# Gate and up projections of a feed-forward block as seven block products, with the weight sums made by accumulating DMAs

## The chip, the cores and the metric

The kernel runs on one core of a Trainium2 chip. A core has five engines that run side by side and meet at semaphores: TensorE (PE in the profile, its weight loads PEld), VectorE (DVE), ScalarE (ACT), GpSimd (POOL) and SyncE (SP, which here only issues DMAs). The metric is the device time of one execution in microseconds (us); of the kernel before there are three runs.

## The reference

One step of a two-layer backbone on 640 tokens: 512 of a sample and 128 of a prompt. Each layer is a token mixer (attention of two kinds, pooling, spatial gating), and then the part that matters here, a SwiGLU feed-forward block:

```python
h = rms_norm(x, p["g_pre_ffn"]) * (1.0 + scale2) + shift2
f = (jax.nn.silu(h @ p["w_gate"]) * (h @ p["w_up"])) @ p["w_down"]
x = x + gate2 * rms_norm(f, p["g_post_ffn"])
```

The model width is 1024, the inner width D_FF is 2816, so `w_gate` and `w_up` are 1024 x 2816 each and `w_down` is 2816 x 1024. All is float32.

## The kernel before

**Precision.** A float32 product is made of three products of the tensor engine in its fp32r format (`mm3`, lines 184 to 189): both operands are split into a high part (ACT, line 125) and a low part (DVE or POOL, line 121), and high x high (L187), high x low (L188) and low x high (L189) are added up in PSUM. `hTh` and `hTl` hold the two parts of the transposed, normed and modulated activations: 8 k-tiles of 128 rows, 640 token columns.

**Gate and up.** `ffn` (from line 949) goes through 22 columns blocks f of 128 inner columns. For each it loads two weight chunks of 512 KB (`raw`, 3 buffers, line 172), one of gate and one of up, and splits each in two halves into `wh` and `wl` (8 buffers of 128x512 each). `product` (line 973) then multiplies them with a stretch of token columns, `HALVES`: first 256 columns, then 384. A stretch of one f is 2 weights x 8 k-tiles x 3 = 48 matmuls. The tanh form of silu follows on ACT (L983) and DVE (L984, L985), and the result is split into `ft`, high and low.

**Down.** The f are taken in three groups of 8, 8 and 6. After each group `w_down` of these f is loaded, and 5 token tiles x 2 halves are multiplied (512 columns each) and added into five rows `acc` (L1020 by ACT for the first group, L1022 by DVE for the others).

**Around it.** The last part of the mixer, `tail(t)`, ends the output projection of token tile t (128 tokens; tiles 0 to 4), norms and transposes it (L355 on PE, two halves per tile) and writes its columns of `hTh`/`hTl`. The first products of the feed-forward block stand in PE's queue between these tails. In layer 0, `mods` computes the modulation of layer 1 in the background of `ffn` (L302 on PE, `w_mod` through chunks of 512 KB).

**Order.** The engines take their instructions strictly in the order that the program's scheduler wrote; a DMA is issued by its queue (SP or POOL) in order too, behind the wait for its buffer. The few lines around the products:

```python
order = [(f, hf) for f in fs for hf in range(2)]
if gi == 0:
    order[:4] = [(0, 0), (1, 0), (0, 1), (1, 1)]
...
for j, p in enumerate(banks):
    for k in range(KT):
        wh, wl = w[f][j][k // 4]
        c = slice((k % 4) * 128, (k % 4 + 1) * 128)
        self.mm3(p[:, :nn], (wh[:, c], wl[:, c]), self.hT(k, n0, nn), k == 0, k == KT - 1)
```

Of the kernel before, what the change touches and what calls it, by code (L numbers as in the profile page):

```python
# [16 lines left out]
NT = 5          # token tiles: 4 of the sample, 1 of the prompt  # L17
# [5 lines left out]
HALVES = [(0, 256), (256, 384)]  # L23
GROUPS = [list(range(0, 8)), list(range(8, 16)), list(range(16, 22))]
# [38 lines left out]
class Kernel:  # L63
# [39 lines left out]
    # PSUM: "s2" tiles are two banks, the others one  # L103
# [26 lines left out]
    def rstd(self, out, ss, n, eps=EPS, more=None):  # L130
        """out = (ss + more + n * eps) ** -0.5: the root of n is left to the factor that follows."""
        if more is None:
            self.V.tensor_scalar(out, ss, n * eps, None, op0=ALU.add)  # L133
        else:
            self.V.tensor_scalar(out, ss, more, n * eps, op0=ALU.add, op1=ALU.add)
        self.G.tensor_tensor(out, out, self.mhalf[:, :out.shape[-1]], op=ALU.pow)  # L136

    def rstd2(self, ss):
        """The same of the sum of two halves of a row."""
        r = self.stat(1, "rs")  # L140
        self.rstd(r, ss[:, 0:1], D, more=ss[:, 1:2])
        return r

# [1 line left out]
    def mark(self, engines):  # L145
        """The instructions traced last on the engines."""
# [88 lines left out]
        # the root of D of the norms' factors  # L235
# [46 lines left out]
    def mod(self, l, pair, al, p, bank, part=0, parts=1):  # L282
        """Two vectors, or a part of them: four products at a time, side by side in the columns of the tensor engine."""
# [30 lines left out]
    def ring(self, slots):  # L314
        """Slots in turn; a slot is a tile or a function that allocates one."""
# [20 lines left out]
    def prestat(self, xt, sq, junk):  # L336
        """1 / rms of the rows of xt."""
# [9 lines left out]
    def pre_t(self, xt, r, i, xr, p):  # L347
        """Half i of the columns of xt * r, transposed, in the bank p; xr is work space."""
# [8 lines left out]

    def modulate(self, l, j, t, i, p, ht, eng):
        """Half i of the contraction: scale and shift, then hi and lo, for the columns of token tile t."""
# [8 lines left out]
        sl = slice(t * 128, (t + 1) * 128)  # L368
        self.split(self.hTh[:, 4 * i:4 * i + 4, sl], self.hTl[:, 4 * i:4 * i + 4, sl], ht, eng)
# [22 lines left out]
    def ytile(self, p, nq=0):  # L392
        """The projection in SBUF, its first nq columns (q of B) scaled."""
# [6 lines left out]
    def rope(self, out, src, cos, sin, ns, hd, tmp, e1, e2, e3):  # L400
        """out = src * cos + swap(src) * sin, ns heads of hd; tables [128, hd]."""
# [12 lines left out]
    def k_stack_b(self, k3):  # L414
        """Stack of k of two heads, k3 [128, 4, 32]: slots h, l, h, l of each."""
# [16 lines left out]
    def prep_b(self, l, t, y):  # L432
        """y: [q | k], 4 heads of 2 x 32 each."""
# [39 lines left out]
    def k_stack_a(self, sk, k, eng):  # L473
        """sk [128, 4, 128]: per head hi twice, lo twice; k [128, 128]."""
# [16 lines left out]
    def prep_a(self, l, t, y):  # L491
        """y: [q of 4 heads | k of 2 | v of 2], 64 columns each."""
# [31 lines left out]
    def att1(self, key, t, rv):  # L524
        """Scores and softmax of query tile t; returns the positions that att2 takes."""
# [53 lines left out]
    def att2(self, key, ts, pos, rv):  # L579
        """Products with the values of one or two positions: two token tiles of a head, or two heads of a tile."""  # L580
# [34 lines left out]
    def subln(self, ts):  # L615
        """Norm of each head of B over its 64 columns, for the token tiles ts."""
# [12 lines left out]
    def pool_a(self, t):  # L629
        """Windows' sums minus count * x, transposed, of a token tile."""  # L630
# [39 lines left out]
    def prep_d(self, t, p):  # L670
        """p: PSUM [u | v] before gelu. u and v are kept doubled."""
# [28 lines left out]
    def mix_t(self, parts, ts, k0):  # L700
        """Transposes of 128 columns of the parts (tensor, column) for the token tiles ts into hT from k0 on."""
# [5 lines left out]
        sl = slice(ts[0] * 128, (ts[-1] + 1) * 128)  # L707
# [7 lines left out]
    def mixer_smalls(self, l):  # L715
# [4 lines left out]
        # lambda  # L720
# [12 lines left out]
        # rotary tables times the q / k norm weights  # L733
# [45 lines left out]
    def mixer_e(self, l, first):  # L779
        """Projections of C, the values and q, k of B, and D; pooling and gating."""  # L780
# [85 lines left out]
    def att(self, key=None, ts=None):  # L866
        """An attention step: the softmax runs LAG steps ahead of the products."""
# [10 lines left out]
    def mixer_t(self, l, xsrc, xdst):  # L878
        """Attention of B and the output projection."""
# [5 lines left out]
        def flush(kind, ts):  # L885
            """Attention steps that have to come before a use of their outputs."""
# [16 lines left out]
        def early(n, t):  # L903
            """Half n of the output projection of token tile t but for B."""
# [6 lines left out]
        def tail(t):  # L911
            """The rest of the output projection, and both norms around its end."""
# [8 lines left out]
            self.mix_t([(self.mixB, 0), (self.mixB, 128)], [t], 2)  # L921
            xt = late["x"][t % (1 + TX)]
            self.SY.dma_start(xt, xsrc(t))
            for n in range(2):
                p = self.p("go"[n if t >= TGO else 0])
                self.gemm_tile(p, t, late["w"][n], [8, 9, 2, 3][2 * EARLY[n]:])
                V.tensor_tensor(m[t][n], p, m[t][n], op=ALU.add)
                S.activation(self.ptile()[:, 0:512], m[t][n], AF.Square, accum_out=ss[:, n:n + 1])
            self.postnorm(m[t], ss, late["g"][t // 4], xt, xdst(t), (self.e("pf"), V if t in GV else G))
            self.prenorm(l, 2, t, xt, self.ptile()[:, 0:512], m[t], "pt" if t in PTT else "s2", self.es("pn"))  # L930

        for x in SEQ.split():
# [12 lines left out]
            elif x[0] == "T":  # L945
                for t in x[1:]:
                    tail(int(t))

    def ffn(self, l, xsrc, xdst, last):
        a, T, V, S, G, pa = self.a, self.T, self.V, self.S, self.G, self.pa  # L950
        big = [self.tl(pa, [128, 3, 1024], tag, n) for tag, n in (("kt", 2), ("kt", 2), ("ka", 1))]
        acc = [big[1][:, 0], big[1][:, 1], big[1][:, 2], big[0][:, 0], big[0][:, 1]]
        rows = [big[2][:, 0], big[2][:, 1]]
        xs = [big[0][:, 2], big[2][:, 2]]
        vb = self.tl(pa, [128, 2, 2, 640], "VB", 1, F32R)
        fts = self.ring([lambda: self.tl(pa, [128, 2, 640], "PT", 4, F32R)] * 4 +
                        [lambda: self.tl(pa, [128, 2, 640], "t5", 3, F32R)] * 3 + [vb[:, 0], vb[:, 1]])

        q = self.tl(pa, [128, 2, 1024], "qa", 1)
        if QX[l]:  # L960
            xs += [q[:, i] for i in range(QX[l])]

        def mods():
            if l == 0:
                al = self.mod_alloc(self.ring([q[:, 0], q[:, 1]] + xs[:2] + rows))
                for pair in ((1, 0), (4, 3), (2, 5)):
                    yield from self.mod(1, pair, al, self.pg(), self.pg)
        bg = mods()
        mark = self.mark([V, G, S])
        for gi, fs in enumerate(GROUPS):  # L970
            ft, w = {}, {}

            def product(f, hf, banks):
                n0, nn = HALVES[hf]
                for j, p in enumerate(banks):
                    for k in range(KT):
                        wh, wl = w[f][j][k // 4]
                        c = slice((k % 4) * 128, (k % 4 + 1) * 128)
# [215 lines left out]
```

## Time and profile before

| what | value |
|---|---|
| runs | 1645.87, 1646.59, 1647.8 us; median 1646.59 |
| span of the profiled execution | 1647.5 us |
| PE busy, matmuls | 1588.7 us (96%), 9643 |
| DVE, ACT, POOL busy | 803.2, 662.9, 389.3 us |
| share of PE in the chain that ended last | 83% |
| DMA | 178.50 MB on SP's queue, 32.1% of the 16 engines |

The profiled execution has no time of its own beside its span; the span lies 0.9 us above the median of the runs and inside their range. "Busy" of PE counts overlapping matmuls once, and their ends are modelled, so the pitch (from start to start) is read from the timeline. The feed-forward blocks lie from about 355 to 860 us (layer 0) and from about 1163 us to the end (layer 1).

### The profile page before, as it was taken

To read this page: it belongs to the slowest core of one execution; us is meant where nothing else is said; L and a number is where in the kernel's file an instruction comes from. 1 tells how busy PE (TensorE), PEld (TensorE's weight loads), DVE (VectorE), ACT (ScalarE), POOL (GpSimd) and SP (SyncE) were. 2 spreads that over 40 slices of the span, in tenths; PEclk is the share of its full clock that TensorE was granted. 3 is DMA by queue.
4 is the path that set the end of the run, shared out by engine and by line. 5 is a ranking of instruction groups with operands and counts; after the bars stand their busy time and mean duration, and the time that the engine had idled before them with its cause. 6 is when DMAs were issued, how large, how long until landed. Compare 5 with 4: busy or idle time off the path is not lost.

```text
span 1647.5 us, 24545 instructions
## 1 busy us (share of the span) xinstructions
PE 1588.7 (96%) x9643; PEld 1362.7 (83%) x9643; DVE 803.2 (49%) x1553; ACT 662.9 (40%) x1472; POOL 389.3 (24%) x338
## 2 busy tenths in 40 slices
PE   7999989999999999999999999998899999999998
PEld 5676767678987989889978877776799889988996
DVE  4557777683231223332376687767723222333335
ACT  5343676563222322222254447765523222212222
POOL 3124214552100211021041242254511021101102
PEclk9999999999999999999999999999999999999999
DMA  9854020255453253122242111102422222213212
GB/s 327 307 179 162 29 84 27 78 185 203 165 205 115 90 192 125 56 97 77 71 164 91 55 61 55 39 26 103 167 90 77 71 84 77 68 49 102 77 65 77
DMA packets 62900, 180.08 MB, mean 109 GB/s; under 512 B 9520, under 2 KB 20784, under 8 KB 62784
## 3 DMA queue, kind: packets, MB, share of 16 engines
q1 hardware_dynamic: 62784, 178.50, 32.1%
q8 instruction: 76, 1.25, 0.3%
q14 instruction: 40, 0.33, 0.1%
HBM read 167.17 MB, written 11.30 MB: 108 GB/s over the span
## 4 chain that ended last, share of the span: by engine, by line
PE 83%; DVE 5%; issue 4%; ACT 4%; POOL 3%; DMA 1%; SPq 0%; DVEq 0%; POOLq 0%; ACTq 0%
PE s L187 8%; PE s L188 8%; PE s L189 8%; PE g L187 6%; PE g L189 6%; PE g L188 6%; PE o L187 5%; PE o L188 5%; PE o L189 5%; PE pt L187 5%; PE pt L188 4%; PE pt L189 4%; PE s L302 2%; PE o L602 2%; PE pt L593 2%
## 5 line engine op out<-in xcount | busy, mean ns | idle before, releaser
L121 DVE TENSOR_TENSOR wl<-raw,wh 128x512 fp32r<-128x512 f32 x240 | 189.0, 795 | 351.3 <-ACT wh L125 348.4
L125 ACT ACTIVATE wh<-raw 128x512 fp32r<-128x512 f32 x344 | 212.1, 631 | 342.9 <-PE s L188 153.6
L121 POOL TENSOR_TENSOR wl<-raw,wh 128x512 fp32r<-128x512 f32 x120 | 164.8, 1379 | 719.4 <-ACT wh L125 717.6
L187 PE MATMUL s<-hTh,wh 128*128 128x384 f32 (+1 forms) x928 | 290.0, 313 | 0.0
L188 PE MATMUL s<-hTl,wh 128*128 128x384 f32 (+1 forms) x928 | 289.0, 311 | 0.0
L189 PE MATMUL s<-hTh,wl 128*128 128x384 f32 (+1 forms) x928 | 288.3, 311 | 0.0
L187 PEld LDWEIGHTS s<-hTh,wh 128*128 128x128 f32 x928 | 174.4, 188 | 6.1 <-ACT P L983 4.2
L189 PEld LDWEIGHTS s<-hTh,wl 128*128 128x128 f32 x928 | 174.6, 188 | 0.0
L188 PEld LDWEIGHTS s<-hTl,wh 128*128 128x128 f32 x928 | 174.2, 188 | 0.2
L187 PE MATMUL pt<-hTh,wh 128*128 128x384 f32 (+1 forms) x448 | 140.1, 313 | 4.0 <-ACT hTh L125 3.9
L188 PE MATMUL pt<-hTl,wh 128*128 128x384 f32 (+1 forms) x448 | 139.6, 312 | 0.0
L189 PE MATMUL pt<-hTh,wl 128*128 128x384 f32 (+1 forms) x448 | 138.8, 310 | 0.0
L187 PE MATMUL g<-wh,hTh 128*128 128x512 f32 x256 | 106.5, 416 | 0.6 <-ACT hTh L125 0.5
L188 PE MATMUL g<-wl,hTh 128*128 128x512 f32 x256 | 103.8, 405 | 0.0
L189 PE MATMUL g<-wh,hTl 128*128 128x512 f32 x256 | 103.3, 404 | 0.4 <-DVE hTl L121 0.4
L136 POOL TENSOR_TENSOR rs<-rs,mhalf 128x1 f32<-128x1 f32 (+3 forms) x66 | 58.2, 885 | 176.8 <-DVE rs L133 126.9
L187 PEld LDWEIGHTS pt<-hTh,wh 128*128 128x128 f32 x448 | 84.5, 189 | 7.7 <-ACT hTh L125 5.1
L547 DVE TENSOR_REDUCE nm<-s 128x1 f32<-128x640 f32 x96 | 77.5, 820 | 27.0 <-PE s L546 13.9
L548 ACT ACTIVATE P<-s,nm 128x640 f32<-128x640 f32 x96 | 76.3, 797 | 28.8 <-DVE nm L547 27.4
L189 PEld LDWEIGHTS pt<-hTh,wl 128*128 128x128 f32 x448 | 84.8, 189 | 0.0
L188 PEld LDWEIGHTS pt<-hTl,wh 128*128 128x128 f32 x448 | 84.4, 188 | 0.3 <-DVE hTl L121 0.3
L984 DVE SCALAR_TENSOR_TENSOR P<-P,s 128x384 f32<-128x384 f32 (+1 forms) x58 | 28.2, 486 | 101.2 <-ACT P L983 101.2
(370 smaller groups left out, 3177.9 us busy)
## 6 DMA issues: line engine op xcount, KB each, us to landing
raw<-in_w_gate SPq DMA_DIRECT2D x44, 512.0 KB
raw<-in_w_up SPq DMA_DIRECT2D x44, 512.0 KB
raw<-in_w_down SPq DMA_DIRECT2D x44, 512.0 KB
kt<-in_w_mod SPq DMA_DIRECT2D x40, 512.0 KB
raw<-in_w_in SPq DMA_DIRECT2D x32, 512.0 KB
ka<-in_w_mod SPq DMA_DIRECT2D x24, 512.0 KB
raw<-in_w_out SPq DMA_DIRECT2D x16, 512.0 KB
qa<-in_w_mod SPq DMA_DIRECT2D x16, 512.0 KB
```

The lines of the kernel that those rows point to most:

```text
L121: eng.tensor_tensor(lo, src, hi.bitcast(F32), op=ALU.subtract)
L125: self.S.activation(hi, src, AF.Copy)
L136: self.G.tensor_tensor(out, out, self.mhalf[:, :out.shape[-1]], op=ALU.pow)
L187: self.T.matmul(out, ah, bh, start=first, stop=False)
L188: self.T.matmul(out, ah, bl, start=False, stop=False)
L189: self.T.matmul(out, al, bh, start=False, stop=last)
L302: self.T.matmul(p[32 * j:32 * j + 32, 0:w], self.c2[:, c:c + 32], raw[k][j // 2][:, j % 2 * w:(j % 2 + 1) * w], start=c == 0, stop=c == 2 ...
L547: V.tensor_reduce(nm[:, s:s + 1], sc[:, :, :320], axis=AX.XY, op=ALU.max, negate=True)
L548: S.activation(P[s].rearrange("p (a b) -> p a b", a=2), sc[:, :, :320], AF.Exp, bias=nm[:, s:s + 1], accum_out=sm[:, s:s + 1])
L593: T.transpose(p[:, j - j0, i * 128:(i + 1) * 128], P[:, j * 128:(j + 1) * 128], self.ident)
L602: T.matmul(o[64 * i:64 * i + 64, 0:128], vt[:, j if nkt == 5 else 5], PT[:, j, i * 128:(i + 1) * 128], start=j == 0, stop=j == nkt - 1)
L984: V.scalar_tensor_tensor(ta, ta, 1.0, gp, op0=ALU.add, op1=ALU.mult)
```

## The change

The 22 blocks f become 11 pairs. Pair 0 is multiplied as before, but with two equal token halves of 320 columns (`HT`). For each of the other ten pairs the product of activations and weights is seen as blocks: the activations A in 2 x 2 (token halves x halves of the 1024 rows), the weights in four blocks b0 to b3 (halves of the rows x the two f of the pair; each block holds gate and up side by side, 128x1024). Instead of eight block products there are seven, numbered 1 to 7, each of 2 banks x 4 k-tiles x 3 matmuls of 320 columns (`product`, new). Their operands are A11 with b0 (product 1), A22-A21 with b0+b1 (5), A12 with b2 (2), a signed sum of A blocks with b0+b1+b3 (6), another with b3 (3), A11-A21 with b1+b3 (7) and A22 with b0+b1+b2+b3 (4); they stand in the order 1, 5, 2, 6, 3, 7, 4, and the 4 of a pair stands behind the 1 of the next.

What this needs beside the products:

- `combine`: the sums of activations, made once per layer on DVE and split by ACT and DVE, for three stretches of columns. For that the token tiles get other columns (`cols`): the first 320 columns hold tiles 0, 1 and the first half of tile 2.
- `blocks`: the sums of weights. `raw` u is loaded with b0 and split; then an accumulating DMA issued by POOL adds b1 to it in place, the sum is split again, b3 is added, split, b2 is added, split. A second `raw` v does b3, then b3+b1. b2 alone comes through two `s` tiles. So a pair has 3 plain loads, 4 accumulating DMAs (512 KB each) and 7 splits of 128x1024, where two f before had 4 loads and 8 splits of 128x512. An accumulating DMA waits for the split ahead of it, and the split behind it waits for the DMA.
- Splits of these weights go to ACT and DVE alone (before, every second low part went to POOL). `wh` and `wl` are 4 buffers of 128x1024 instead of 8 of 128x512.
- In `middle` and `end`: five additions of 128x640 on DVE per pair, PSUM to SBUF (L1138, L1163), between the products and the silu (`swiglu`, L1063 to L1066).
- Four groups for the down projection (2, 3, 3, 3 pairs) instead of three; `w_down` and, in layer 0, `w_mod` come through the eight `s` tiles of 128x512 (before: 512 KB chunks), the latter spread over groups 1 to 3, three steps per pair (`mod_s`).

```diff
-HALVES = [(0, 256), (256, 384)]
-GROUPS = [list(range(0, 8)), list(range(8, 16)), list(range(16, 22))]
+HT = TOK // 2
+GROUPS = [[0, 1], [2, 3, 4], [5, 6, 7], [8, 9, 10]]
...
+    def piece(self, src):
+
+        h, l = self.wtile()
+        for x in src:
+            c, y = x
+            self.split(h[:, c], l[:, c], y, self.V)
+        return h, l
+
+    def blocks(self, l, pair):
+
+
+        SY, G = self.SY, self.G
+        blk = [self.a["w_gu"][l, pair, q] for q in range(4)]
+        full = slice(0, 1024)
+        wraw = lambda: self.tl(self.wp, [128, 1024], "raw", 3)
+        add = lambda o, q: G.dma_start(o, blk[q], accum_op=ALU.add)
+        u = wraw()
+        SY.dma_start(u, blk[0])
+        yield self.piece([(full, u)])
+        add(u, 1)
+        yield self.piece([(full, u)])
+        z = [self.s() for _ in range(2)]
+        for i in range(2):
+            SY.dma_start(z[i], blk[2][:, i * 512:(i + 1) * 512])
+        add(u, 3)
+        yield self.piece([(slice(i * 512, (i + 1) * 512), z[i]) for i in range(2)])
+        yield self.piece([(full, u)])
+        add(u, 2)
+        v = wraw()
+        SY.dma_start(v, blk[3])
+        yield self.piece([(full, v)])
+        add(v, 1)
+        yield self.piece([(full, v)])
+        yield self.piece([(full, u)])
...
+            V.tensor_tensor(a22, a22, a21, op=ALU.subtract)
+            self.split(*out(5), a22, V)
+            V.tensor_tensor(a21, a11, a21, op=ALU.subtract)
+            V.scalar_tensor_tensor(a11, a22, -1.0, a11, op0=ALU.mult, op1=ALU.subtract)
+            self.split(*out(6), a11, V)
+            self.split(*out(7), a21, V)
+            V.scalar_tensor_tensor(a12, a12, -1.0, a11, op0=ALU.mult, op1=ALU.subtract)
+            late.append((out(3), a12))
...
+    def product(self, n, w, banks, first=True, last=True):
+
+        ah, al = self.ops[n]
+        wh, wl = w
+        for j, p in enumerate(banks):
+            o = p[:, 0:HT]
+            for k in range(4):
+                c = slice(j * 512 + k * 128, j * 512 + (k + 1) * 128)
+                a, b = (wh[:, c], wl[:, c]), (ah[:, k, :], al[:, k, :])
+                self.T.matmul(o, a[0], b[0], start=first and k == 0, stop=False, skip_group_check=True)
+                self.T.matmul(o, a[0], b[1], start=False, stop=False, skip_group_check=True)
+                self.T.matmul(o, a[1], b[0], start=False, stop=last and k == 3, skip_group_check=True)
...
+            self.product(5, next(w), [b[:, 0], b[:, 1]], last=False)
+            add(wt, b, x)
+            self.product(2, next(w), aa, first=False)
+            self.swiglu(t1[:, n1], aa[0][:, n1], aa[1][:, n1], 1, 0)
+            next(bg, None)
+            self.product(6, next(w), [c[:, 0], c[:, 1]], last=False)
+            add(yt, c, x)
+            next(bg, None)
+            self.product(3, next(w), [b[:, 0], b[:, 1]], first=False)
+            add(yt, b, yt)
+            self.swiglu(t2[:, n1], yt[:, n1], yt[:, n2], -1, 0)
+            next(bg, None)
+            self.product(7, next(w), [c[:, 0], c[:, 1]], first=False, last=False)
+            add(wt, c, wt)
+            self.swiglu(t2[:, n2], wt[:, n1], wt[:, n2], -1, 1)
...
+            for pair in ps:
+                if pair == 0:
+                    continue
+                nst = begin(pair)
+                if st:
+                    end(st)
+                st = nst
+                middle(st, bg)
```

Two places show how instructions move. The first is PE at the start of the feed-forward block of layer 0: `s_762`/`s_810` are the transposes of token tile 2, `pt_37..` those of tile 3, `o_37..` the end of tile 4's and 3's output projection, and `s_799`/`s_851` the first gate product. Before:

```order
L355 MATMUL s_810_3679<-identr_77,s_2500 128x128 x4
L189 MATMUL o_3803<-wh_3431,hTl_89 128x512
L187 MATMUL s_851_3884<-hTh_88,wh_3865 128x256
L188 MATMUL s_851_3884<-hTl_89,wh_3865 128x256
L189 MATMUL s_851_3884<-hTh_88,wl_3866 128x256
...
L355 MATMUL pt_3756<-identr_77,s_2502 128x128 x4
L355 MATMUL pt_3757<-identr_77,s_2503 128x128 x3
L355 MATMUL s_810_3679<-identr_77,s_2501 128x128 x4
L355 MATMUL pt_3757<-identr_77,s_2503 128x128
L189 MATMUL s_851_3884<-hTh_88,wl_3880 128x256
```

and now:

```order
L371 MATMUL s_762_3631<-identr_77,s_2468 128x128 x4
L192 MATMUL o_3755<-wh_3381,hTl_89 128x512
L371 MATMUL pt_3708<-identr_77,s_2470 128x128 x4
L371 MATMUL pt_3709<-identr_77,s_2471 128x128 x4
L371 MATMUL s_762_3631<-identr_77,s_2469 128x128 x4
L190 MATMUL s_799_3834<-hTh_88,wh_3813 128x320
L190 MATMUL g_3890<-hTh_88,wh_3824 128x320
L190 MATMUL o_3891<-hTh_88,wh_3824 128x320
L191 MATMUL s_799_3834<-hTl_89,wh_3813 128x320
```

Before, 41 products of 256 columns stood ahead of the transposes of tile 3; now all transposes of tiles 2 and 3 stand ahead of the first product, which reads columns of tile 2.

The second place is DVE in the middle of a group, layer 0. Before, a pair of low parts of weights (`wl`) stands between the silu of one stretch and the next, each waiting for a chunk that depends on nothing else:

```order
L121 TENSOR_TENSOR wl_4595<-raw_4588,wh_4594 128x512
L121 TENSOR_TENSOR wl_4605<-raw_4598,wh_4604 128x512
L984 SCALAR_TENSOR_TENSOR P_4421<-P_4421,s_902_4372 128x384
L985 SCALAR_TENSOR_TENSOR P_4421<-P_4421,s_902_4372 128x384
L121 TENSOR_TENSOR PT_4315<-P_4421,PT_4315 128x384
L984 SCALAR_TENSOR_TENSOR P_4509<-P_4509,s_915_4460 128x256
```

Now, with `raw_4787` the u of one pair and `raw_5073` that of the next (L1138 adds a product from PSUM):

```order
L121 TENSOR_TENSOR wl_5031<-raw_4983,wh_5030 128x1024
L121 TENSOR_TENSOR wl_5076<-raw_5073,wh_5075 128x1024
L1138 TENSOR_TENSOR P_4858<-s_926_4856,P_4786 128x640
L121 TENSOR_TENSOR wl_5106<-raw_4787,wh_5105 128x1024
L1138 TENSOR_TENSOR P_4858<-s_925_4855,P_4858 128x640
L121 TENSOR_TENSOR wl_5149<-raw_5073,wh_5148 128x1024
L1064 SCALAR_TENSOR_TENSOR P_4860<-P_4860,P_4858 128x320
L1066 SCALAR_TENSOR_TENSOR P_4860<-P_4860,P_4858 128x320
L1138 TENSOR_TENSOR P_4857<-s_926_4856,P_4857 128x640
```

`wl_5076` is the split for product 1 of the next pair; the accumulating DMA of b1 goes out behind it, and `wl_5149`, which waits for that DMA, stands three rows on, ahead of the addition that frees the bank of product 7 (`s_926`) for product 4. On POOL nothing but these DMAs is left inside the feed-forward block, in order (x3: three on the same u):

```order
L996 DMA raw_4787<-in_w_gu 128x1024 x3
L996 DMA raw_4983<-in_w_gu 128x1024
L996 DMA raw_5073<-in_w_gu 128x1024 x3
L996 DMA raw_5269<-in_w_gu 128x1024
L996 DMA raw_5652<-in_w_gu 128x1024 x3
```

Before, POOL made half of the low parts of weights there.

## Rows read from the trace of the kernel before

**Rows 1.** The page: busy time by engine; the last chain by engine.

```profile
PE 1588.7 (96%) x9643; PEld 1362.7 (83%) x9643; DVE 803.2 (49%) x1553; ACT 662.9 (40%) x1472; POOL 389.3 (24%) x338
...
PE 83%; DVE 5%; issue 4%; ACT 4%; POOL 3%; DMA 1%; SPq 0%; DVEq 0%; POOLq 0%; ACTq 0%
```

**Rows 2.** Stretches: length, PE, PEld, DVE, ACT, POOL busy, clock, DMA share, GB/s.

```profile
0.00:60.00 60.00, 49.54 (x423) 34.54 (x424) 28.16 (x75) 27.84 (x62) 19.30 (x25) 1.00 0.97 321
...
360.00:840.00 480.00, 478.49 (x2899) 428.82 (x2898) 152.39 (x271) 138.83 (x265) 70.00 (x54) 1.00 0.38 131
```

**Rows 3.** PE's groups by line and shape: count, busy us, mean ns.

```profile
L187 PE MATMUL s<-hTh,wh 128*128 128x384 f32 x480 | 162.7, 339 | 0.0
...
L187 PE MATMUL s<-hTh,wh 128*128 128x256 f32 x448 | 127.4, 284 | 0.0
```

**Rows 4.** PE's timeline, layer 0: start, us, line, operands, shape.

```profile
525.33 0.40 PE L189 MATMUL o<-wh,PT 128*128 128x512 f32 x1
...
546.33 0.40 PE L187 MATMUL g<-wh,VB 128*128 128x512 f32 x1
...
548.16 0.28 PE L187 MATMUL s<-hTh,wh 128*128 128x256 f32 x1
...
553.20 0.28 PE L187 MATMUL s<-hTh,wh 128*128 128x256 f32 x1
...
553.73 0.34 PE L187 MATMUL s<-hTh,wh 128*128 128x384 f32 x1
...
558.50 0.34 PE L187 MATMUL s<-hTh,wh 128*128 128x384 f32 x1
```

**Rows 5.** Timelines of PE, ACT and DVE at the start of layer 0's block.

```profile
355.20 0.28 PE L187 MATMUL s<-hTh,wh 128*128 128x256 f32 x1
...
361.36 0.98 PE L355 MATMUL pt<-identr,s 128*128 128x128 f32 x7 [1.08 <-DVE s L352]
...
364.11 0.69 DVE L121 TENSOR_TENSOR hTl<-s,hTh 128x512 fp32r<-128x512 f32 x1
...
370.33 1.15 ACT L125 ACTIVATE hTh<-s 128x512 fp32r<-128x512 f32 x2
...
371.04 2.71 POOL L121 TENSOR_TENSOR hTl<-s,hTh 128x512 fp32r<-128x512 f32 x2 [3.19 <-ACT hTh L125]
...
371.98 1.46 PE L302 MATMUL g<-ka,c 128*32 128x512 f32 x10
```

**Rows 6.** The same place in layer 1: timelines, PE's longest wait, one stretch.

```profile
1162.93 0.36 PE L187 MATMUL s<-hTh,wh 128*128 128x256 f32 x1
...
1173.15 0.62 ACT L125 ACTIVATE hTh<-s 128x512 fp32r<-128x512 f32 x1
...
1180.16 0.63 ACT L125 ACTIVATE hTh<-s 128x512 fp32r<-128x512 f32 x1
...
PE pt L187 <- ACT hTh L125: 3.9, 1, 3.9
...
1180.00:1185.00 5.00, 1.94 (x6) 1.94 (x7) 3.16 (x8) 3.49 (x9) 3.62 (x3) 0.75 0.15 57
```

**Rows 7.** Instructions on `raw` (ns min/median/max), DVE groups (count, busy us, mean ns).

```profile
L121 DVE TENSOR_TENSOR wl<-raw,wh x240: 676/693/1798, 20.0 to 1619.7; 128x512 fp32r<-128x512 f32 x120
...
L573 DVE SCALAR_TENSOR_TENSOR P<-P,rb,P 128x640 f32<-128x640 f32 x24 | 23.6, 984 | 1.0
...
L984 DVE SCALAR_TENSOR_TENSOR P<-P,s 128x384 f32<-128x384 f32 x30 | 16.4, 548 | 0.0
...
L984 DVE SCALAR_TENSOR_TENSOR P<-P,s 128x256 f32<-128x256 f32 x28 | 11.8, 421 | 101.2 <-ACT P L983 101.2
```

**Rows 8.** Two 512 KB loads: issue on SP, and the ACT split that waited.

```profile
1482.21 0.33 SPq L172 DMA_DIRECT2D raw<-in_w_down  x1
...
1485.87 1.16 ACT L125 ACTIVATE wh<-raw 128x512 fp32r<-128x512 f32 x2 [1.62 <-DMA raw<-in_w_down]
...
23.19 0.34 SPq L172 DMA_DIRECT2D raw<-in_w_in  x1
...
30.90 1.15 ACT L125 ACTIVATE wh<-raw 128x512 fp32r<-128x512 f32 x2 [1.36 <-DMA raw<-in_w_in]
```

**Rows 9.** The page: the only DMA queue of loads: packets, MB, share.

```profile
q1 hardware_dynamic: 62784, 178.50, 32.1%
```

More of the change, by code (lines that the diff above doesn't have):

```diff
@@ L329, in mod_alloc, with mod_s @@
         return al
+    def mod_s(self, l, pair, p, bank):
+        src = self.a["w_mod"][l].rearrange("(k p) (i n) -> p k i n", p=128, n=D)
+        for k in range(KT):
+            for j in range(4):
+                raw = self.s()
+                self.SY.dma_start(raw, src[:, k, pair[j // 2], j % 2 * 512:(j % 2 + 1) * 512])
+                self.T.matmul(p[32 * j:32 * j + 32], self.c2[:, 2 * k:2 * k + 32], raw, start=k == 0, stop=k == KT - 1)
+            yield
+        self.mod_finish(l, pair, 512, 0, p, lambda what: self.s(), bank)
+        yield
     def row(self, l, i, c, tile_):
@@ L947, in mixer_t @@
                     tail(int(t))
-    def ffn(self, l, xsrc, xdst, last):
-        a, T, V, S, G, pa = self.a, self.T, self.V, self.S, self.G, self.pa
[L951 to L978, printed above, removed]
-                        self.mm3(p[:, :nn], (wh[:, c], wl[:, c]), self.hT(k, n0, nn), k == 0, k == KT - 1)
-                gp, up = (p[:, :nn] for p in banks)
-                ta = self.ptile()[:, :nn]
-                sl = slice(n0, n0 + nn)
-                S.activation(ta, gp, AF.Tanh, scale=0.5)
-                V.scalar_tensor_tensor(ta, ta, 1.0, gp, op0=ALU.add, op1=ALU.mult)
-                V.scalar_tensor_tensor(ta, ta, 0.5, up, op0=ALU.mult, op1=ALU.mult)
-                self.split(ft[f][:, 0, sl], ft[f][:, 1, sl], ta)
-            order = [(f, hf) for f in fs for hf in range(2)]
-            if gi == 0:
-                order[:4] = [(0, 0), (1, 0), (0, 1), (1, 1)]
-                first = list(FIRST)
-                self.n3 = 2
-            for f, hf in order:
-                if hf == 0:
-                    w[f] = [self.chunk(a[nme][l, f], self.es("wg")) for nme in ("w_gate", "w_up")]
-                    ft[f] = next(fts)
-                product(f, hf, self.pair(first.pop(0) if first else ("s2", "s2", "pt")[self.n3 % 3]))
-                self.n3 += 1
-                if hf:
-                    self.step(bg, PACE, mark)
-            lastg = gi == len(GROUPS) - 1
-            if lastg:
-                self.step(bg, 99, mark)
-                rows = [self.row(l, 5, c, rows[c]) for c in range(2)]
@@ new lines, in combine, with rest @@
+    def combine(self, m):
+        V = self.V
+        kt = [self.tl(self.pa, [128, 2, 4, HT], "kt", 2, F32R) for _ in range(2)]
+        s3 = [self.tl(self.pa, [128, 4, HT], "PT", 4, F32R) for _ in range(2)]
+        h, lo = self.hTh, self.hTl
+        self.ops = {1: (h[:, 0:4, 0:HT], lo[:, 0:4, 0:HT]), 2: (h[:, 4:8, 0:HT], lo[:, 4:8, 0:HT]),
+                    3: (h[:, 0:4, HT:TOK], lo[:, 0:4, HT:TOK]), 4: (h[:, 4:8, HT:TOK], lo[:, 4:8, HT:TOK]),
+                    5: (kt[0][:, 0], kt[0][:, 1]), 6: (kt[1][:, 0], kt[1][:, 1]), 7: s3}
+        late = []
+        for c, t1, t2 in ((256, 2, 2), (0, 0, 3), (128, 1, 4)):
+            n = 64 if t1 == 2 else 128
+            q = lambda t, i, o: m[t][i].rearrange("p (k n) -> p k n", n=128)[:, :, o:o + n]
+            o2 = 64 if t1 == 2 else 0
+            a11, a12, a21, a22 = q(t1, 0, 0), q(t1, 1, 0), q(t2, 0, o2), q(t2, 1, o2)
+            out = lambda k: [x[:, :, c:c + n] for x in self.ops[k]]
+            V.tensor_tensor(a22, a22, a21, op=ALU.subtract)
[6 more added lines that the diff above has]
+            late.append((out(3), a12))
+        def rest():
+            for o, x in late:
+                self.split(*o, x, V)
+        return rest
@@ L1005, in ffn @@
                 ss = [self.stat(2, "ss2") for _ in range(NT)]
             for n in range(2):
[L1007 removed]
+                w = []
+                for pair in ps:
+                    h, lo = self.wtile()
+                    for i in range(2):
+                        c = slice(i * 512, (i + 1) * 512)
+                        x = self.s()
+                        self.SY.dma_start(x, a["w_down"][l, n, pair][:, c])
+                        self.split(h[:, c], lo[:, c], x, V)
+                        w.append((h[:, c], lo[:, c]))
```

151 lines of the change are left out of this document (128 added, 23 removed).

## Prediction

> **What bounds the kernel now.** The busy times and the last chain came first [rows 1]: PE is busy 96% of the span and is 83% of the chain that ended last, and no other engine passes 49%. So time follows from the columns that PE works through, as long as nothing makes it wait. The stretches come second [rows 2]: in the feed-forward block of layer 0 PE works 478.49 of 480 us, at a full granted clock, with the DMA engines at 0.38. The groups by shape [rows 3] tell how much of that is gate and up: 448 to 480 matmuls a line in these two groups alone; with the other PSUM tags there are 704 of each shape in each of the three lines (11 pairs, 2 layers, 2 f, 2 weights, 8 k), so 2112 of 256 columns and 2112 of 384. The means there (284 and 339 ns) count the drain of a pipelined matmul, so the pitch must come from the timeline [rows 4]: (553.20−548.16)/42 = 0.120 us for 256 columns, (558.50−553.73)/27 = 0.177 for 384, (546.33−525.33)/90 = 0.233 for 512. The pitch is proportional to the columns within 3%.
>
> **What is removed and added on PE.** 320 columns do not occur among these rows; I take the mean of 256 and 384, 0.148 us. (From below 0.146, 512's rate; from above 0.150, 256's; over the 3744 matmuls counted next that is ±8 us.) Before: 2112 × (0.120+0.177) = 626 us. After: pair 0 has 2 halves × 2 f × 2 weights × 24 = 192 matmuls a layer, 28.4 us, 57 us for both. A product has 24 matmuls, 3.56 us, and a pair seven, 24.9 us; 20 pairs are 497 us. Together 554: **72 us less**, 3.6 for each of the 20 pairs. Columns for the down projection and the modulation stay.
>
> **The engines behind it.** DVE per pair: 7 low parts of 128x1024, 14 × 0.693 = 9.7 us; five additions of 640 columns at about 0.85 (below the 0.984 of a three-operand one) 4.3; silu, eight instructions of 320 columns at about 0.485, 3.9; low parts of the result 1.8 [rows 7]. That is 19.7 of 24.9 us, high but no bound. ACT: 7 × 1.16 = 8.1 for the high parts [rows 8] and about 4 for the rest. POOL loses its splits. What gets thin is the lead: the split weights hold four products, 14.2 us, where eight chunks held 28.5.
>
> **The accumulating DMAs.** No such DMA is in the trace: SP's queue is the only one with loads [rows 9]. The question is A, from the end of a split to the landing of the sum. From below it is a plain 512 KB load at a quiet place, 1485.87−1482.21 = 3.66 us; among many loads 30.90−23.19 = 7.7 [rows 8]. From above, twice that, 15.4. A second read of 512 KB takes 1.5 us at the engines' rate: 131/0.38 = 345 GB/s, and 321/0.97 = 331 [rows 2], over the whole run 178.5 MB/(0.321 × 1647.5 us) = 337 [rows 9]. I take 3.7+1.5 and some 0.8 for issue by POOL: A = 6 quiet, 8.5 beside `w_mod`.
>
> The Trainium skill gives a price for the plain transfer: "DMA: Bandwidth & Descriptors", section "Anatomy of one DMA — SWDGE (gpsimd) path", 2.0 us and bytes/436 GB/s, so 3.2 us for 512 KB as an estimate, 0.5 under the quiet row here. "Collectives: The Full Stack", under "Why ReduceScatter is half of AllGather", says that an add is held to half rate because it reads two sources on one ring; that would make 4.4 us of it, with which no pair would stall and the sum below would be 1598. No row here shows either.
>
> How much A can hide: the split for the next pair's product 1 finds its buffer free when product 2 has ended. Product 4 follows four products later (6, 3, 7 and the next 1), 14.2 us. Between lie that split (1.16 on ACT, 1.39 on DVE), A, the split of the sum (2.55), two steps of silu (1.0) and the addition that frees product 7's bank for product 4 (1.0), since DVE works strictly in order. 14.2−7.1 leaves **A up to 7.1 us hidden**; each us more costs one per pair. At 3.6 us gain per pair, an A of about 10.7 takes all of it.
>
> So layer 1 hides the adds (6 against 7.1). In the nine pairs of layer 0 with `w_mod`, a pair moves 7 × 0.524 MB of weights, 12 × 0.262 of `w_mod`, and 4 × 0.524 read back for the sums: 8.9 MB in 24.9 + 12 × 0.146 [rows 5] = 26.6 us, 335 GB/s, the capacity above. Hence 8.5 there: 1.4 over, 9 pairs, **13 us lost**.
>
> **The start of the block.** Before, PE had 96 products of 256 columns, 11.5 us, that need tiles 0 and 1 alone; it ran them from 355.20 while tiles 2 to 4 were normed [rows 5]. Now the first product reads half of tile 2. That tile's first half is split low by 364.80; the second, by the high part at 370.33 and the low part behind it, is ready near 372. With the first half 48 matmuls can run, 7.1 us, so 4.4 of the 11.5 are bared; the place also holds 2.8 us of modulation (ten take 1.46) and late low parts such as POOL's, 3.19 late. I take 8 us. In layer 1 products began at 1162.93, the halves are split near 1173.8 and 1181, and before PE waited 3.9 us there too, after which the clock was granted at 0.75 [rows 6]; 11.5−7.1 = 4.4, I take 5. **13 us lost**, from 6 (all but the bared part hidden) to 20 (no product before the second half, 11.5 in each, less 3).
>
> **First pairs and groups.** In each layer the first of the seven-product pairs finds its buffers still held by pair 0, and its chain of split, A, split runs bare in part: 3 us each, **6 us** (0 to 2 × 8.5). A fourth group adds a round of waits and ten additions of 512 columns on DVE, up to 7 us; in the third group's stretch down matmuls stood in step [rows 4], so it can be 0; **4 us**.
>
> **Sum.** −72+13+13+6+4 = −36. Against the profiled 1647.5 that is 1611.5; this execution lies 0.9 us above the median of the runs, which gives **1611**.
>
> **Rivals.**
> *The adds cost nothing.* If A stays under 7.1 also beside `w_mod` and the first pairs are covered: −72+13+4 = −55, 1592. For it: the engines have 0.38 share now, and the quiet load is 3.66. Against: 335 GB/s in those pairs.
> *The engines saturate in layer 0.* If a sum takes their time three times (source, old value, write), a pair needs 11.0 MB, at 345 GB/s 31.9 us, 5.3 more than PE: 48 us instead of 13, about 1646, no change. For it: in the first 60 us the share was 0.97 and PE was idle for 10 of them [rows 2]. Against: the 0.38 was counted with each byte once, so reads and writes seem to overlap.
> *Slow adds, the other side.* If issue on POOL and the sum make A 12 us everywhere, then 5 us of stall in 18 pairs, 90 instead of 13 and 6: about 1682, slower. It decides from A = 10.5. For it: 7.7 for a plain load under load, and each pair chains three sums on one buffer. Against: POOL has nothing else to do there. The skill bears on this rival with "DMA: Bandwidth & Descriptors", section "SWDGE vs HWDGE vs iDMA": descriptors from GpSimd are written by it into SBUF, where VectorE in its two-port mode can lock it out. No row here shows it.
> *The pitch of 320 is no mean.* Weight loads average 1362.7/9643 = 0.141 us [rows 1], hardly under 0.148; if they showed, all 3744 matmuls would be dearer. But 256 columns go at 0.120 with the same loads [rows 4], so it is worth at most the 8 us above.
>
> **Chances.** The sum as worked out 0.45, free adds 0.2, saturation 0.15, slow adds 0.18; 0.02 for the rest. The first case has 1590 to 1630 of its own (start 6 to 20, pitch ±8, taken together). The range must also hold the first two rivals: 1586 to 1655; slow adds are left out. A measurement of this kernel tells 0.2% (3.3 us) from no change. Faster: 0.45+0.2 and a third of saturation and a little, 0.71; same 0.07; slower 0.22.
>
> **What would show it.** Right: gate and up matmuls at a pitch near 0.148 and products of 3.56 us back to back in layer 1; a PE wait of some us ahead of the first product in each layer, ended by ACT or DVE on tile 2; short waits before product 4 in layer 0's pairs with `w_mod`, ended by the chain from a POOL DMA; A of 6 and 8.5. Wrong: PE waits of over 3.6 us in every pair, in layer 1 too (A over 10.5); a DMA share near 1 through layer 0's block (saturation); DVE above 90% there, with additions, not splits, ending PE's waits.

## The result: slower, with the adds as cheap as forecast

The changed kernel takes 1714.19 us (median of 4 runs, 1710.76 to 1715.36), the kernel before 1646.23 beside it: ratio 1.0397, interval 1.0378 to 1.0417. The forecast was 1611, with 1586 to 1655 as the range and a chance of 0.22 for slower. The slow-adds rival (1682) has the right sign, but not the right reason, as the rows show.

From the page of the changed kernel: busy times, the queue of POOL's DMAs, and the DMA issues with their median from issue to landing.

```profile
PE 1565.2 (91%) x9163; PEld 1314.6 (77%) x9163; DVE 1002.8 (59%) x1825; ACT 721.7 (42%) x1508; POOL 347.5 (20%) x330
...
q0 software_dynamic: 11520, 41.95, 13.8%
...
raw<-in_w_gu POOLq DMA_DIRECT2D x80, 512.0 KB, 6.0
raw<-in_w_gu SPq DMA_DIRECT2D x48, 512.0 KB, 3.7
```

Beside [rows 1], PE is busy 23.5 us less, where 72 were forecast, and idle 147.8 us of 1713.0 instead of 58.8 of 1647.5. The accumulating DMA, POOL's row, takes 6.0 us in the median, just what was taken for the quiet case.

Where did PE wait? Three rows of PE's waits, over the whole span: who ended them, total us, times, longest.

```profile
PE s L1056 <- ACT wh L125: 25.6, 14, 5.0
PE s L1056 <- DVE P L1138: 18.9, 12, 2.4
...
PE pt L1056 <- ACT wh L125: 8.7, 4, 4.4
```

L1056 is the first matmul of each three of a product. The waits end with the high part of a weight sum (ACT) or with an addition (DVE) that stands behind a split in DVE's queue. What those wait for shows in one pair of layer 1, where no `w_mod` is loaded. ACT's splits of `raw` and POOL's DMAs, from one split of product 7 to the next (start, us, xcount, idle time before and its releaser), then the stretch as in [rows 2]:

```profile
1346.00 2.96 ACT L125 ACTIVATE wh<-raw 128x1024 fp32r<-128x1024 f32 x3 [4.37 <-DMA raw<-in_w_gu]
1356.01 1.06 ACT L125 ACTIVATE wh<-raw 128x1024 fp32r<-128x1024 f32 x1 [7.05 <-DMA raw<-in_w_gu]
1364.42 1.06 ACT L125 ACTIVATE wh<-raw 128x1024 fp32r<-128x1024 f32 x1 [3.60 <-DMA raw<-in_w_gu]
1366.69 1.05 ACT L125 ACTIVATE wh<-raw 128x1024 fp32r<-128x1024 f32 x1
1376.11 1.06 ACT L125 ACTIVATE wh<-raw 128x1024 fp32r<-128x1024 f32 x1 [4.54 <-DMA raw<-in_w_gu]
...
1349.86 0.90 POOL L996 DMA_DIRECT2D raw<-in_w_gu  x1 [8.78 <-DVE wl L121]
1358.73 0.89 POOL L996 DMA_DIRECT2D raw<-in_w_gu  x1 [7.97 <-DVE P L1064]
1367.14 0.88 POOL L996 DMA_DIRECT2D raw<-in_w_gu  x1 [7.53 <-DVE wl L121]
1370.15 0.88 POOL L996 DMA_DIRECT2D raw<-in_w_gu  x1 [2.13 <-DVE P L1064]
...
1346.00:1376.10 30.10, 26.13 (x172) 24.96 (x171) 17.18 (x26) 10.80 (x17) 3.53 (x4) 1.00 0.54 122
```

Read it as a chain. At 1346.00 ACT splits, one behind the other, the weights of products 7, next 1 and 4. The split of next 1 lets b1 go out at 1349.86; its sum is split for product 5 at 1356.01 (6.15 us). That lets b3 go out at 1358.73, split for 6 at 1364.42 (5.69). Behind it, ACT splits v for product 3 at 1366.69; that lets b1 go out into v at 1370.15, split for 7 at 1376.11 (5.96), and only behind that, in the order of ACT, stands the split for the next product 1. So a turn is **three accumulating DMAs in a row**, 17.8 us, and 12.3 us of splits and order between them: 30.11 us, where PE has work for 24.7 (shown below, in the kernel without a chain). PE is busy 26.13 of these 30.10 us, at a granted clock of 1.00. The fourth DMA, of 1367.14, lies beside the third.

In layer 0 the DMAs take longer beside `w_mod` (8.2 and 9.1 us, from issue to split, around the waits below). There, a wait can cost twice (PE's timeline around product 5 of one pair and product 4 of the pair before, then the stretch, and layer 0 as in [rows 2]):

```profile
655.71 0.31 PE L1058 MATMUL pt<-hTh,wl 128*128 128x320 f32 x1
...
657.03 0.31 PE L1058 MATMUL pt<-hTh,wl 128*128 128x320 f32 x1
659.77 0.64 PE L1056 MATMUL s<-kt,wh 128*128 128x320 f32 x1 [2.43 <-ACT wh L125]
...
662.69 0.63 PE L1056 MATMUL s<-hTh,wh 128*128 128x320 f32 x1 [2.02 <-DVE P L1138]
663.12 0.47 PE L1057 MATMUL s<-hTl,wh 128*128 128x320 f32 x1
663.39 0.47 PE L1058 MATMUL s<-hTh,wl 128*128 128x320 f32 x1
...
659.00:666.00 7.00, 4.21 (x14) 3.81 (x15) 5.38 (x10) 3.97 (x8) 0.86 (x1) 0.53 0.69 175
...
360.00:840.00 480.00, 441.18 (x2572) 384.35 (x2572) 239.20 (x381) 157.35 (x259) 43.83 (x46) 0.96 0.58 157
```

After the waits of 2.43 and 2.02 us the pitch is 663.39−663.12 = 0.27 us instead of (657.03−655.71)/9 = 0.147: the granted clock of that stretch is 0.53, so close to its lower level of 1.2 GHz. Over the same 480 us as in [rows 2], PE is busy 441.18 us instead of 478.49 and the mean clock 0.96 instead of 1.00.

### The profile page after: what moved, and what is told of

Its sections match the earlier page's. It is cut to its first block, busy times and chain, and to the rows that moved or that the text cites. A ratio compares the mean times of both kernels' runs of the same rounds, so it can differ in the third digit from the quotient of the medians.

```text
span 1713.0 us, 24194 instructions
## 1 busy us (share of the span) xinstructions
PE 1565.2 (91%) x9163; PEld 1314.6 (77%) x9163; DVE 1002.8 (59%) x1825; ACT 721.7 (42%) x1508; POOL 347.5 (20%) x330
## 3 DMA queue, kind: packets, MB, share of 16 engines
q1 hardware_dynamic: 76608, 168.02, 28.5%
q0 software_dynamic: 11520, 41.95, 13.8%
## 5 line engine op out<-in xcount | busy, mean ns | idle before, releaser
L121 DVE TENSOR_TENSOR wl<-raw,wh 128x1024 fp32r<-128x1024 f32 (+1 forms) x192 | 208.3, 1102 | 297.6 <-ACT wh L125 297.3
L125 ACT ACTIVATE wh<-raw 128x1024 fp32r<-128x1024 f32 (+1 forms) x208 | 177.5, 889 | 380.1 <-DMA raw<-in_w_gu 265.1
L1056 PE MATMUL s<-kt,wh 128*128 128x320 f32 x320 | 101.9, 318 | 19.0 <-ACT wh L125 18.9
L1056 PE MATMUL s<-hTh,wh 128*128 128x320 f32 x320 | 104.6, 327 | 12.2 <-DVE P L1138 11.1
L1056 PE MATMUL pt<-hTh,wh 128*128 128x320 f32 x320 | 101.4, 317 | 8.8 <-ACT wh L125 8.7
L1058 PE MATMUL s<-kt,wl 128*128 128x320 f32 x320 | 99.8, 312 | 4.4 <-DVE wl L121 4.4
L1058 PE MATMUL s<-hTh,wl 128*128 128x320 f32 x320 | 102.4, 320 | 0.8 <-DVE wl L121 0.7
L1057 PE MATMUL s<-hTl,wh 128*128 128x320 f32 x320 | 102.2, 319 | 0.0
L1057 PE MATMUL pt<-hTl,wh 128*128 128x320 f32 x320 | 100.6, 315 | 0.0
L1057 PE MATMUL s<-kt,wh 128*128 128x320 f32 x320 | 99.5, 311 | 0.0
L1056 PEld LDWEIGHTS s<-kt,wh 128*128 128x128 f32 x320 | 60.4, 189 | 29.6 <-ACT wh L125 21.8
L1056 PEld LDWEIGHTS s<-hTh,wh 128*128 128x128 f32 x320 | 63.6, 199 | 23.1 <-DVE P L1138 12.9
```

What stands on the lines that cost most here:

```text
L121: eng.tensor_tensor(lo, src, hi.bitcast(F32), op=ALU.subtract)
L125: self.S.activation(hi, src, AF.Copy)
L1056: self.T.matmul(o, a[0], b[0], start=first and k == 0, stop=False, skip_group_check=True)
L1057: self.T.matmul(o, a[0], b[1], start=False, stop=False, skip_group_check=True)
L1058: self.T.matmul(o, a[1], b[0], start=False, stop=last and k == 3, skip_group_check=True)
```

## The experiments

**Theories.** The chain: a pair can't be shorter than three accumulating DMAs in a row and the splits between them. VectorE: it has 59% of the span instead of 49%, works in order, and ends a third of the waits above; its amount of work is what costs. Traffic: the second read of the sums fills the DMA engines in layer 0. And the prediction's own reading: only the DMA between next product 1 and next product 5 counts, and 7 us of it are hidden.

**No add, same places** (the sums are left out):

```diff
-        add = lambda o, q: G.dma_start(o, blk[q], accum_op=ALU.add)
+        add = lambda o, q: G.dma_start(o, blk[q])
```

> The four DMAs that POOL issues per pair load their block without adding it, into the same buffers and behind the same splits; the sums of weights are left out. Chain theory: a pair's period is three of these DMAs in a row plus about 12.3 us of splits between them (29.7 us in layer 1 now, with 5.6 to 6.2 us each from issue to split). If a plain one takes 4.5 us, the period is 25.8 in layer 1, just above the 24.9 of PE, and the time falls from 1714 to about 1640 to 1655. VectorE theory (PE waits because VectorE takes its splits and additions in one order and has too many of them): that work is unchanged, so the time stays at 1705 to 1715. Traffic theory (the second read of the sums fills the DMA engines in layer 0): layer 0 alone gains, some 45 us, layer 1 keeps its 29.7 us periods: about 1670.

Measured: 1618.9 us (1618.67 to 1625.75), ratio 0.9833 [0.9806, 0.9859]. From its page:

```profile
q0 software_dynamic: 11520, 41.95, 7.7%
...
raw<-in_w_gu POOLq DMA_DIRECT2D x80, 512.0 KB, 4.1
```

And the first matmul of the first and of the last product 7 in layer 1:

```profile
1218.19 0.31 PE L1056 MATMUL s<-PT,wh 128*128 128x320 f32 x1
...
1562.14 0.31 PE L1056 MATMUL s<-PT,wh 128*128 128x320 f32 x1
```

The DMA from POOL takes 4.1 us instead of 6.0, and 95 us go; the order on PE, VectorE, ScalarE and GpSimd is that of the changed kernel. More than expected, since 4.1 is under the 4.5 that was assumed. VectorE's theory fails, as its work is unchanged (1004.7 us). The traffic theory fails too: between these two products 7 of layer 1 lie 344.0 us, where the changed kernel has 389.2 (its lines stand under "Why the prediction was wrong"), while in layer 0 this distance falls by 34.7.

**No chain** (the sums are left out; every split has a buffer that SP loads plain):

```diff
-        u = wraw()
-        SY.dma_start(u, blk[0])
-        yield self.piece([(full, u)])
-        add(u, 1)
-        yield self.piece([(full, u)])
+        def one(q):
+            u = wraw()
+            SY.dma_start(u, blk[q])
+            return self.piece([(full, u)])
+        yield one(0)
+        yield one(1)
...
```

> Every one of the seven splits reads a block that SyncE loaded plain into a buffer of its own turn; no DMA waits for the split before it, and the sums of weights are left out. All matmuls, splits and additions on VectorE stay. Chain theory: PE sets the pairs again, 24.9 us in layer 1 and about 28.5 with its modulation in layer 0; the 90 us or so of waits and slow clock inside the groups go: 1610 to 1630. VectorE theory: 1700 to 1715. Traffic theory: layer 0 gains up to 45 us, layer 1 nothing: about 1670.

Measured: 1597.37 us (1596.36 to 1598.97), ratio 0.9689 [0.9675, 0.9704]; below what any theory gave, nearest to the chain. Its busy times, a stretch of layer 1, and the first matmul of product 7 in two pairs of it:

```profile
PE 1523.0 (95%) x9163; PEld 1289.1 (81%) x9163; DVE 1007.8 (63%) x1825; ACT 725.8 (45%) x1508; POOL 276.1 (17%) x250
...
1258.00:1310.00 52.00, 52.00 (x355) 51.90 (x354) 38.46 (x60) 24.56 (x40) 0.00 (x0) 1.00 0.44 151
...
1258.24 0.31 PE L1051 MATMUL s<-PT,wh 128*128 128x320 f32 x1
1282.89 0.30 PE L1051 MATMUL s<-PT,wh 128*128 128x320 f32 x1
```

A pair takes 24.65 us here, PE doesn't stop in this stretch, and VectorE has the same work as in the changed kernel (1007.8 against 1002.8), 74% of the stretch. This kernel also tells what the adds and the waits for them cost in all: 1713.0−1595.7 = 117.3 us, of which 147.8−72.7 = 75.1 are idle time of PE and 1565.2−1523.0 = 42.2 are busy time of PE for the same 9163 matmuls. The lower clock is a part of these 42.2: the mean granted clock is 0.963 in the changed kernel and 0.982 here, which is at most 0.037 × 1713.0 − 0.018 × 1595.7 = 34.7 us. The rest was not taken apart.

**Another order** (nothing left out): the next pair's product 1, with its split and DMA, stands ahead of product 7. For that, the sums of b1 into u and into v are also issued ahead of products 1 and 3 instead of behind them.

```diff
-        yield self.piece([(full, u)])
+        w = self.piece([(full, u)])
         add(u, 1)
+        yield w
...
             next(bg, None)
+            nst = begin(nxt) if nxt else None
             self.product(7, next(w), [c[:, 0], c[:, 1]], first=False, last=False)
...
```

> Product 1 of the next pair, and with it its split and accumulating DMA, stands ahead of product 7 of this pair in the program (order 1, 5, 2, 6, 3, next 1, 7, 4); nothing is added or left out. Chain theory: the DMA for product 7 and that for the next product 5 then run side by side, and the period is two DMAs and about 9 us: 21 us in layer 1, 25 in layer 0, under PE's 24.9 and 28.5. The time falls to 1620 to 1645. VectorE theory: same work, other order: within 10 us of 1714. If each DMA could hide 7 us as the prediction had it, the order would also not matter: 1714.

Measured: 1642.83 us (1640.1 to 1644.82), ratio 0.9963 [0.995, 0.9976]; inside what the chain theory gave, near its upper end, 71 us under the changed kernel. ACT and POOL in layer 1:

```profile
1308.32 1.06 ACT L125 ACTIVATE wh<-raw 128x1024 fp32r<-128x1024 f32 x1 [1.52 <-PE s L1059]
1313.60 1.06 ACT L125 ACTIVATE wh<-raw 128x1024 fp32r<-128x1024 f32 x1 [3.23 <-DMA raw<-in_w_gu]
1318.63 1.06 ACT L125 ACTIVATE wh<-raw 128x1024 fp32r<-128x1024 f32 x1 [2.46 <-PE s L1059]
...
1307.28 0.88 POOL L996 DMA_DIRECT2D raw<-in_w_gu  x1 [1.34 <-DVE wl L121]
1311.56 0.90 POOL L996 DMA_DIRECT2D raw<-in_w_gu  x1 [3.40 <-DVE P L1066]
```

The split for next 1 (1308.32) no longer waits for the sum for 7 (issued 1307.28, split 1313.60), and it and the one for next 5 (1318.63) wait for a buffer that PE frees, no more for a DMA. The two sums run side by side.

**GpSimd adds** (nothing left out): the blocks come into spare `s` tiles by SP, and GpSimd adds them.

```diff
-        add = lambda o, q: G.dma_start(o, blk[q], accum_op=ALU.add)
+        def add(o, q):
+            for i in range(2):
+                c, y = slice(i * 512, (i + 1) * 512), self.s()
+                SY.dma_start(y, blk[q][:, c])
+                G.tensor_tensor(o[:, c], o[:, c], y, op=ALU.add)
```

> The blocks to be added are loaded by SyncE into spare 128x512 tiles ahead of time, and GpSimd adds them, two additions of 128x512 per sum, in the place of the accumulating DMA; order as in the change. GpSimd's subtractions of that shape took 1.38 us before, so a sum takes about 2.9 us. Chain theory: period 3 x 2.9 + 12.3 = 21 us, under PE's: 1615 to 1640. VectorE theory: 1710 or more, since VectorE's work stays and GpSimd's reads lie beside it.

Measured: 1643.47 us (1641.93 to 1648.86), ratio 0.9977 [0.9965, 0.9989]; 3 us outside what was expected, but 71 gained. A sum takes GpSimd about 3 us (160 additions at 1.57 us in the mean, two to a sum). VectorE is busier than in the changed kernel, 1070.0 against 1002.8 us, and still the time falls, which speaks once more against its theory. In layer 1 the products 7 of a group lie 24.36 to 24.84 us apart, PE's own pace; what is left over lies in layer 0, with mostly 33 us where the kernel without a chain has 28. Unlike in the run without the add, other instructions moved too, on PE, VectorE and ScalarE. Both edits of sums and order together:

> The two edits together: next product 1 ahead of product 7, and sums by GpSimd from blocks loaded ahead, instead of accumulating DMAs; nothing is left out. Each alone gave 1643. Chain theory: the loop is then two sums of 2.9 us and 9 us of splits, 15 us, far under PE's 24.9; what is left over the kernel without a chain (1597) is the w_mod stretch of layer 0, where the tiles of the blocks come late, some 2 us per pair: 1600 to 1625. If the two edits had removed the same waits, it would stay near 1640.

Measured: 1621.71 us (1620.57 to 1621.93), ratio 0.9843 [0.9829, 0.9858]: faster than both kernels. In layer 1 it runs like the kernel without a chain: from the first product of the block to the end both take 440 us. The 24 us between them lie ahead of that. In layer 0's block GpSimd waits 125.7 us for tiles of the blocks (DMA `s<-in_w_gu`), in layer 1's 11.9, as the expectation had it; that these waits make the 24 us was not tested.

**One sum of four.** The DMA into v (in the row) or the last one into u (beside the row) becomes a plain load; the one sum is left out, and the order on every engine is that of the changed kernel.

```diff
-        add(v, 1)
+        G.dma_start(v, blk[1])
```

> Of the four accumulating DMAs per pair, the one into the second buffer (for product 7) becomes a plain load, in the same place and the same order of all engines; that one sum is left out. The kernel with all four plain took 4.1 us for one instead of 6.0. Chain theory: this DMA is one of the three in a row, so each pair gains about 2 to 3 us and a third of the 95 us of that kernel is had: 1675 to 1692. The prediction's own reading (only the DMA between next product 1 and next product 5 lies on the path): 1714, no change.

Measured: 1684.8 us (1681.24 to 1686.17), ratio 1.0225 [1.0209, 1.024]: 29 us gained, inside what the chain theory gave.

```diff
-        add(u, 2)
+        G.dma_start(u, blk[2])
```

> The same exchange for another of the four: the last one into the first buffer (for product 4), which lies beside that of product 7 and not in the row. Same edit, same saving of traffic, same order of the engines; that one sum is left out. Chain theory: 1705 to 1714, nearly nothing. If any saved accumulation helped alike (traffic, issue on GpSimd's queue), it would equal the run with product 7's made plain.

Measured: 1697.81 us (1695.44 to 1700.32), ratio 1.0304 [1.0286, 1.0322]: 16 us gained, not the nothing that was expected. The turns of layer 1 tell why; first v plain, then b2 plain, then b2 plain and the changed kernel where the two DMAs go out together:

```profile
1328.56 2.95 ACT L125 ACTIVATE wh<-raw 128x1024 fp32r<-128x1024 f32 x3 [2.40 <-DMA raw<-in_w_gu]
1356.46 1.06 ACT L125 ACTIVATE wh<-raw 128x1024 fp32r<-128x1024 f32 x1 [2.33 <-DMA raw<-in_w_gu]
```

```profile
1337.23 2.95 ACT L125 ACTIVATE wh<-raw 128x1024 fp32r<-128x1024 f32 x3 [4.31 <-DMA raw<-in_w_gu]
1367.22 1.06 ACT L125 ACTIVATE wh<-raw 128x1024 fp32r<-128x1024 f32 x1 [4.54 <-DMA raw<-in_w_gu]
...
1433.84 0.56 POOL L1008 DMA_DIRECT2D raw<-in_w_gu  x1 [9.08 <-DVE wl L121]
1434.97 0.89 POOL L996 DMA_DIRECT2D raw<-in_w_gu  x1 [0.56 <-DVE P L1064]
1440.93 2.00 ACT L125 ACTIVATE wh<-raw 128x1024 fp32r<-128x1024 f32 x2 [4.87 <-DMA raw<-in_w_gu]
```

```profile
1441.16 0.88 POOL L996 DMA_DIRECT2D raw<-in_w_gu  x1 [9.02 <-DVE wl L121]
1442.30 0.88 POOL L996 DMA_DIRECT2D raw<-in_w_gu  x1 [0.26 <-DVE P L1064]
1449.22 2.00 ACT L125 ACTIVATE wh<-raw 128x1024 fp32r<-128x1024 f32 x2 [5.84 <-DMA raw<-in_w_gu]
```

In the turn read above (30.11 us), v plain gives 27.90, and b2 plain 29.99, nothing: there the two go out 3 us apart. Where they go out 1.1 us apart, the sum in v takes 6.92 us in the changed kernel and 5.96 with b2 plain. That holds over all 20 pairs: in the 16 where the two go out within 2.2 us, the sum in v takes 7.10 us in the mean, from issue to split, and 6.16 with b2 plain, which over 16 turns makes 15 us, about what was gained; in the other four it takes 6.15 and 5.98. So b2 is not in the row; it slows the sum that is.

**One sum doubled** (b1 is added to v twice):

```diff
         add(v, 1)
+        add(v, 1)
```

> The accumulating DMA for product 7 is issued twice, one behind the other, so that block is added twice. Chain theory: about 6 us more in each of the pairs where the chain binds, 14 to 18 of 20: 1800 to 1830. The prediction's own reading, in which this DMA has slack: 1714 to 1730.

Measured, a single run: 1843.56 us, 129 us more, 6.5 for each of the 20 pairs in the mean, and above the 1800 to 1830 that were expected. The distances from one product 7 to the next in a layer, those across the end of a group too, all grow, by 0.9 to 10.7 us; the prediction's reading, with slack there, fails. The order of other instructions changed with the added DMA, so this run alone would not settle it.

## Why the prediction was wrong

**The step that failed** is "How much A can hide": "A up to 7.1 us hidden; each us more costs one per pair". It followed one sum, from next product 1 to product 4, through DVE's order, and took the beginning of that split as free once its buffer was. It is not: it stands behind the split for product 7, which waits for a sum of its own, which waits behind two more. With the forecast's own figures the turn is 3 × 6 for the sums and five splits of 2.55 between them, 30.8 us; measured, 17.8 + 12.3. PE has 24.7. That the two come so near is in part luck: the three stretches between the sums measure 3.86 us (splits of 7 and next 1), 2.72 (5) and 5.73 (6 and 3), where splits of 2.55 in a row would give 5.1, 2.55 and 5.1. So an A of 6 is not hidden but 5 us too long per pair, an A of 4 is about what fits, and each us costs three per pair. Break-even stood at an A of 10.7; by this turn it is estimated near 5.4 (3 × 5.4 + 12.3 = 28.5, what a pair took before), with no price for the clock in it. The prediction's sign of being wrong, PE waits of over 3.6 us per pair in layer 1 too, came true inside the groups (4.0 us in the turn read above), but it was tied to an A over 10.5, and A is 6.

**The terms.** The adds were costed at 13 us in layer 0, 6 in the first pairs and nothing in the other pairs of layer 1; they cost 117.3. Where, tells the comparison of the first product of 320 columns and the first and last product 7 of each layer. Changed kernel, then no chain:

```profile
364.06 0.61 PE L190 MATMUL s<-hTh,wh 128*128 128x320 f32 x1
...
420.73 0.31 PE L1056 MATMUL s<-PT,wh 128*128 128x320 f32 x1
...
830.52 0.31 PE L1056 MATMUL s<-PT,wh 128*128 128x320 f32 x1
...
1210.29 0.63 PE L190 MATMUL s<-hTh,wh 128*128 128x320 f32 x1
...
1268.07 0.47 PE L1056 MATMUL s<-PT,wh 128*128 128x320 f32 x1
...
1657.25 0.47 PE L1056 MATMUL s<-PT,wh 128*128 128x320 f32 x1
```

```profile
362.29 0.62 PE L190 MATMUL s<-hTh,wh 128*128 128x320 f32 x1
...
410.93 0.31 PE L1051 MATMUL s<-PT,wh 128*128 128x320 f32 x1
...
777.69 0.31 PE L1051 MATMUL s<-PT,wh 128*128 128x320 f32 x1
...
1155.48 0.64 PE L190 MATMUL s<-hTh,wh 128*128 128x320 f32 x1
...
1205.04 0.31 PE L1051 MATMUL s<-PT,wh 128*128 128x320 f32 x1
1539.76 0.31 PE L1051 MATMUL s<-PT,wh 128*128 128x320 f32 x1
```

Pairs: 409.8 against 366.8 us in layer 0 and 389.2 against 334.7 in layer 1, together 97.5 lost; layer 1, costed at nothing, loses more. First pairs, up to product 7: 56.7 against 48.6 and 57.8 against 49.6, together 16.3 (forecast 6). The rest is within 4 us.

**What held.** The seven products: a pair takes 24.65 us without a chain (forecast 24.9). A: 6.0 in the median (6 quiet, 8.5 with `w_mod`; there, in the timeline of layer 0, 8.2 and 9.1 in the pair of the wait above). VectorE is no bound: it keeps up when PE never stops. The other terms, −72, 13 for the start and 4 for the fourth group, make −55; the kernel without a chain has 1595.7−1647.5 = −51.8. This is also the first rival's 1592, which needed adds that cost nothing. Of the 13 at the start, layer 0's first product stands 8.9 us later (364.06 against 355.20 in [rows 5]), near the 8 taken (this compares where the block begins, not what it costs); layer 1's part was not taken apart.

**The rivals.** Slow adds: the sign and the order of size, but by a DMA of 12 us, which it is not. Saturation: not the cause, since layer 1, with a DMA share of 0.43 from 1210 us on, loses more than layer 0. What the prediction called against slow adds, that POOL has nothing else to do, holds; that "each pair chains three sums on one buffer", named for it, was nearly the right place (the row is two sums on u and one on v), and was not followed into a sum.

**The price of an add.** The Trainium skill, "Collectives: The Full Stack", under "Why ReduceScatter is half of AllGather", says that the add there needs two source reads and pushes twice the read traffic through one ring. The engines' time here agrees: the same 41.95 MB take 13.8% of the engines with the add and 7.7 without, 13.8 × 1713.0 against 7.7 × 1616.9, 1.9 times. As a price of the latency, the 4.4 us that the prediction worked out from it were too low: 6.0 with the add against 4.1 without.

## What to carry to other kernels

If a buffer is split, added to and split again in place, write the whole turn down as a cycle: every transfer that waits for a split, and every split that only stands behind another in its engine's order; the period is their sum, and a latency that looks hidden in one link counts as often as it occurs. Here latency in a turn was bought back by order (start the next turn ahead of the last wait of this one) or by an engine that adds what is loaded already; each gave 71 us and both 92. Here a saving of 72 us of matmuls bought nothing as long as the feed's period was above the new, shorter one of the matmuls.

## What the runs showed that was not expected

A 512 KB accumulating DMA into SBUF takes 6.0 us from POOL, a plain one from POOL 4.1, and one from SP 3.7. The later of two accumulating ones that go out within 2.2 us takes 7.1 us to the split, and 6.2 when the earlier one is plain. And waits inside the pairs can cost a second time through the granted clock: over the 7 us with the waits of 2.43 and 2.02 us it was 0.53, while in the turn read above, with 4.0 us of waits, it stayed at 1.00. At most 35 of the 117 us are the lower clock.
